# Weight halves that are stationary, interleaved column by column, and begun at eight places in turn

## The chip, the cores and the metric

The kernel runs on one core of a Trainium2 chip. The metric is the time of one execution on the device in microseconds (us); of several runs the median is given. Matrix products run on TensorE (PE in the profile, with its weight loads as PEld), elementwise work on VectorE (DVE), ScalarE (ACT) and GpSimd (POOL), and transfers are issued from SyncE's queue (SP) and GpSimd's.

## The reference, cut to what matters

Two transformer-like blocks run on 512 tokens of width 2048, in fp32: the first has differential attention and a state-space branch, the second has two layers with neighbourhood, dilated and memory attention. Nearly all arithmetic is in products of the activations with large weights:

```python
# first block, once
h = rms_norm(x, ln_gain[l])
proj = h @ w_in[l]                                # 512 x 2048 times 2048 x 10240
q, k, v, z_att, u, z_ssm, g_att, g_ssm = jnp.split(proj, splits, axis=-1)
...                                               # attention, S5 scan
return y * jax.nn.sigmoid(y @ w_glu + b_glu)
...
merged = (jax.nn.sigmoid(g_att) * (y_att @ w_proj_att[l])
          + jax.nn.sigmoid(g_ssm) * (y_ssm @ w_proj_ssm[l]))
x = x + merged @ w_out[l]

# second block, two layers, on x and on mem (256 rows)
h = rms_norm_2(x, norm_g[l])
z = h @ w_in[l]                                   # 2048 x 7168
...                                               # three kinds of attention, gates
x = x + y @ w_out[l]
```

## The kernel before, in words

Activations lie transposed in SBUF, 16 tiles of 128 features by 512 tokens. Each is kept as two halves in the type fp32r: a high half that the type holds exactly, and the rest as a low half. Weights are split in the same way, and a product of a weight block and an activation tile is three matmuls into one PSUM tile (`mm3`, lines 183 to 185): high by high, high by low, low by high.

Weights come in units (`wunit`): four blocks of 128 rows by 256 columns, one DMA of 512 KB into `raw` (line 196), a cast to the high half on ScalarE (`split`, line 189) and a subtraction for the low half on VectorE (line 190), both over 1,024 elements in each of 128 partitions. The result is `hl`, in a ring of three buffers; a buffer holds 2,176 elements and the halves take 2,048 of them, so that the place where they begin (`at`, in bytes) can be chosen. The high halves of all four blocks lie first, and the low halves behind them: a row of a block is 256 elements without a gap. A unit is asked for ahead of time by the scheduler's priority, and begins when the matmuls on the unit three before it have given their buffer back.

Two kinds of product use the units. In `gemm_t` the weight is the stationary operand, in pieces of 128 columns, and the activations move, 512 columns (256 where the memory of 256 rows is the activation); the result comes out transposed, in two PSUM tiles `pg`. In `gemm_tok` the activations are stationary and the weights move, 256 columns at a time. Both go through `accumulate`, which takes the units one after the other; a unit of `gemm_t` is 4 blocks x 2 pieces x 3 = 24 matmuls. The constants `AT_T, AT_MEM, AT_TOK = 256, 64, 448` say where in the buffer the halves begin for 512 columns, for the memory's 256, and for `gemm_tok`.

Between the matmuls of these products, `tick` lets pieces of other work in by a count that is written in the code (`SSM_EVERY`, `ATT_EVERY` and such): attention scores (L848, L849), transposes of weights of attention (L1132), sums of squares by a matmul with a constant (L779, stationary `blk64` and `onesE`), and the state-space branch. Its scan (63 steps of five small VectorE instructions, L564 to L568) runs beside products with `w_in`. What the change touches is `wunit`, `gemm_t`, `gemm_tok` and `accumulate`.

Of the kernel before, what the change touches and what calls it, by code (L numbers as in the profile page):

```python
# [20 lines left out]
NMEM = 256  # L21
# [22 lines left out]
AT_T, AT_MEM, AT_TOK = 256, 64, 448  # L44
# [73 lines left out]
class Net:  # L118
    def __init__(self, ctx, tc, a):
        self.ctx, self.tc, self.nc, self.a = ctx, tc, tc.nc, a  # L120
        self.n = 0
        self.between = []
        self.ahead = AHEAD_FIRST
        nc = self.nc
        cp = ctx.enter_context(tc.tile_pool(name="const", bufs=1))
        self.cp = cp
        self.ident = self.const("ident", [P, P])
        self.onesD = cp.tile([P, P], F32, name="onesD")
        nc.vector.memset(self.onesD, 1.0 / D)
        self.col = ctx.enter_context(tc.tile_pool(name="col", bufs=16))  # L130

        line = ctx.enter_context(tc.tile_pool(name="line", bufs=1, side="right"))
        line.tile([P, 120], F32, name="line")
        self.wr = ctx.enter_context(tc.tile_pool(name="wr", bufs=3))
        self.wh = ctx.enter_context(tc.tile_pool(name="wh", bufs=3))
        self.tmp = ctx.enter_context(tc.tile_pool(name="tmp", bufs=8))
        self.nrm = ctx.enter_context(tc.tile_pool(name="nrm", bufs=2))
        self.pg = ctx.enter_context(tc.tile_pool(name="pg", bufs=4, space=PSUM))
        self.pa = ctx.enter_context(tc.tile_pool(name="pa", bufs=2, space=PSUM))
        self.dram = ctx.enter_context(tc.tile_pool(name="scratch", bufs=1, space=DRAM))  # L140
# [48 lines left out]
        self.nc.scalar.copy(hi, src)  # L189
        self.nc.vector.tensor_sub(lo, src, hi.bitcast(F32))  # L190

    def wunit(self, src, k0, kk, c0, cw=256, pool=None, at=0):

        with self.tc.high_priority(self.ahead):
            raw = self.wr.tile([P, 4, 256], F32, tag="raw", name=self.nm("raw"))[:, :kk, :cw]
            self.nc.sync.dma_start(out=raw, in_=src[k0 * P:(k0 + kk) * P, c0:c0 + cw].rearrange("(k p) c -> p k c", p=P))
            hl = (pool or self.wh).tile([P, 2176], FR, tag="hl", name=self.nm("hl"), bufs=4 if pool else 3)
            hl = hl[:, at // 4:at // 4 + 2048].rearrange("p (h k c) -> p h k c", h=2, k=4)[:, :, :kk, :cw]
            self.split(hl[:, 0], hl[:, 1], raw)
        return hl  # L200

# [21 lines left out]
    def gemm_t(self, src, c0, mov, n=T):  # L223

        out = [self.psg()[:, :n] for _ in range(2)]

        def step(hl, k, kk, i, first, last):
            x = mov[k]
            c = slice(i * P, (i + 1) * P)
            self.mm3(out[i], hl[:, 0, kk, c], hl[:, 1, kk, c], x[:, 0], x[:, 1], first, last)  # L230

        return self.accumulate(src, c0, len(mov), out, step, AT_MEM if n == NMEM else AT_T)

    def gemm_tok(self, src, c0, mov, nt):

        out = [self.psg()[:, :256] for _ in range(nt)]

        def step(hl, k, kk, i, first, last):
            x = mov[k]
            t = slice(i * P, (i + 1) * P)  # L240
            self.mm3(out[i], x[:, 0, t], x[:, 1, t], hl[:, 0, kk], hl[:, 1, kk], first, last)

        return self.accumulate(src, c0, len(mov), out, step, AT_TOK)

    def accumulate(self, src, c0, kt, out, step, at):


        n = len(out)
        for ku in range(0, kt, 4):
            hl = self.wunit(src, ku, 4, c0, at=at)  # L250
            order = [(k, i) for k in range(4) for i in range(n)]
            if ku == 0:
                order.sort(key=lambda o: o[1] // 2)
            if ku == kt - 4:
                order.sort(key=lambda o: o[1])
            for k, i in order:
                step(hl, ku + k, k, i, ku + k == 0, ku + k == kt - 1)
                self.tick(1.0 / n)
        return out
# [1008 lines left out]
```

## Time and profile before

| what | value |
|---|---|
| median of 3 runs | 3312.57 us (3311.8 to 3313.15) |
| the profiled execution's own time | 3314.32 us |
| its span, first to last instruction | 3312.3 us |
| TensorE matmuls busy | 3275.6 us (99%), 17,844 instructions |
| TensorE weight loads busy | 2823.8 us (85%) |
| VectorE busy | 1753.0 us (53%) |
| ScalarE busy | 1174.2 us (35%) |
| GpSimd busy | 293.3 us (9%) |
| DMA | 410.11 MB, 124 GB/s on average |

The profile is of one execution. Busy time counts an engine as occupied while any instruction of it runs; matmuls are pipelined and overlap, so the duration of one is longer than the distance from its start to the next one's, and it is the distances that add up to the span. Rows name the engine, the line of the kernel, and the tiles by the program's names: `pg<-xg,hl` is a matmul into `pg` with moving operand `xg` and stationary `hl`.

### The profile page before, as it was taken

What the parts mean: (1) busy time and instruction counts of PE and PEld (TensorE: products, weight loads), DVE (VectorE), ACT (ScalarE), POOL (GpSimd) and SP (SyncE); (2) the same over time, 40 slices, a digit from 0 to 9 for tenths busy, and PEclk for the clock granted to TensorE, in tenths of its full rate; (3) what the DMA queues carried; (4) which work ended last, traced back from release to release, by engine and by line L of the source; (5) the groups of instructions that cost most, each with busy time, mean ns of one, the idle gap of its engine ahead of it and who ended that gap; (6) DMA issues with size and microseconds to landing.
All of it is one profiled execution on the core that took longest, in us unless ns stands there. A gap on an engine that the chain in (4) does not pass through costs nothing.

```text
span 3312.3 us, 44959 instructions
## 1 busy us (share of the span) xinstructions
PE 3275.6 (99%) x17844; PEld 2823.8 (85%) x17844; DVE 1753.0 (53%) x3227; ACT 1174.2 (35%) x1851; POOL 293.3 (9%) x426
## 2 busy tenths in 40 slices
PE   8999999999999999999999999999999999999998
PEld 6998877888888788888888888888888888888898
DVE  5464486445888754434444556443354455554433
ACT  4432222243555432223333334323343333343333
POOL 3200001311111000011011000001101100000000
PEclk9999999999999999999999999999999999999999
DMA  6564443454333354344333222334443332233433
GB/s 222 180 199 120 130 123 121 135 187 134 100 101 96 110 186 146 124 141 153 99 98 94 90 87 76 127 122 132 147 138 96 95 93 86 83 97 123 137 113 111
DMA packets 365954, 410.11 MB, mean 124 GB/s; under 512 B 36506, under 2 KB 327209, under 8 KB 365616
## 3 DMA queue, kind: packets, MB, share of 16 engines
q1 hardware_dynamic: 350800, 363.73, 35.4%
q0 software_dynamic: 14944, 43.52, 3.7%
q8 instruction: 140, 2.29, 0.3%
q14 instruction: 70, 0.57, 0.1%
HBM read 355.86 MB, written 47.70 MB: 122 GB/s over the span
## 4 chain that ended last, share of the span: by engine, by line
PE 94%; DVE 3%; DMA 1%; issue 1%; ACT 0%; POOL 0%; SPq 0%; ACTq 0%; DVEq 0%; POOLq 0%
PE pg L183 29%; PE pg L185 28%; PE pg L184 28%; PE pa L1132 1%; PE pa L184 1%; PE pa L185 1%; PE pa L183 1%; DVE hl L190 1%; PE pa L584 0%; DVE s L565 0%; DVE s L566 0%; DVE s L567 0%; DVE st L568 0%; DVE s L564 0%; PE pa L779 0%
## 5 line engine op out<-in xcount | busy, mean ns | idle before, releaser
L190 DVE TENSOR_TENSOR hl<-raw,hl 128x1024 fp32r<-128x1024 f32 x552 | 680.8, 1234 | 943.9 <-ACT hl L189 942.4
L183 PE MATMUL pg<-xg,hl 128*128 128x512 f32 (+1 forms) x2688 | 1069.7, 398 | 0.0
L185 PE MATMUL pg<-xg,hl 128*128 128x512 f32 (+1 forms) x2688 | 1039.9, 387 | 8.8 <-DVE hl L190 8.8
L184 PE MATMUL pg<-xg,hl 128*128 128x512 f32 (+1 forms) x2688 | 1038.1, 386 | 0.0
L189 ACT CAST hl<-raw 128x1024 fp32r<-128x1024 f32 x552 | 578.9, 1050 | 1074.5 <-PE pg L185 890.5
L185 PEld LDWEIGHTS pg<-xg,hl 128*128 128x128 f32 x2688 | 505.6, 188 | 115.2 <-DVE hl L190 13.8
L183 PEld LDWEIGHTS pg<-xg,hl 128*128 128x128 f32 x2688 | 507.4, 189 | 87.7 <-ACT xg L312 0.4
L184 PEld LDWEIGHTS pg<-xg,hl 128*128 128x128 f32 x2688 | 507.7, 189 | 80.4
L183 PE MATMUL pg<-hl,xg 128*128 128x256 f32 x1152 | 327.4, 284 | 0.0
L185 PE MATMUL pg<-hl,xg 128*128 128x256 f32 x1152 | 322.3, 280 | 0.0
L184 PE MATMUL pg<-hl,xg 128*128 128x256 f32 x1152 | 322.2, 280 | 0.0
L184 PE MATMUL pg<-yh,hl 128*128 128x512 f32 x576 | 224.3, 389 | 0.0
L185 PE MATMUL pg<-yh,hl 128*128 128x512 f32 x576 | 224.3, 389 | 0.0
L183 PE MATMUL pg<-yh,hl 128*128 128x512 f32 x576 | 224.3, 389 | 0.0
L185 PEld LDWEIGHTS pg<-hl,xg 128*128 128x128 f32 x1152 | 219.0, 190 | 0.0
L183 PEld LDWEIGHTS pg<-hl,xg 128*128 128x128 f32 x1152 | 217.0, 188 | 1.5
L184 PEld LDWEIGHTS pg<-hl,xg 128*128 128x128 f32 x1152 | 216.7, 188 | 1.6
L183 PE MATMUL pg<-hl,yh 128*128 128x256 f32 x512 | 145.7, 285 | 0.0
L190 DVE TENSOR_TENSOR wt<-pa,wt 128x512 fp32r<-128x512 f32 (+3 forms) x144 | 83.1, 577 | 118.2 <-ACT wt L189 117.7
L185 PE MATMUL pg<-hl,yh 128*128 128x256 f32 x512 | 143.7, 281 | 0.0
L184 PE MATMUL pg<-hl,yh 128*128 128x256 f32 x512 | 143.6, 281 | 0.0
L189 ACT CAST wt<-pa 128x512 fp32r<-128x512 f32 (+3 forms) x144 | 71.3, 495 | 166.6 <-PE pa L1132 166.2
(282 smaller groups left out, 3983.0 us busy)
## 6 DMA issues: line engine op xcount, KB each, us to landing
raw<-in_w_in_dram SPq DMA_DIRECT2D x384, 512.0 KB, 3.5
raw<-in_w_out_dram SPq DMA_DIRECT2D x96, 512.0 KB, 3.6
raw<-in_w_mem_kv_dram SPq DMA_DIRECT2D x32, 512.0 KB, 4.5
o_d<-t POOLq DMA_DIRECT2D x40, 256.0 KB, 2.3
t<-o_d SPq DMA_DIRECT2D x40, 256.0 KB, 3.9
sg_d<-t POOLq DMA_DIRECT2D x32, 256.0 KB, 2.5
raw<-in_w_proj_att_dram SPq DMA_DIRECT2D x16, 512.0 KB, 3.7
raw<-in_w_proj_ssm_dram SPq DMA_DIRECT2D x16, 512.0 KB, 3.6
```

Of the source, the lines that this page charges most:

```text
L183: mm(ps, wh, xh, start=start, stop=False)
L184: mm(ps, wh, xl, start=False, stop=False)
L185: mm(ps, wl, xh, start=False, stop=stop)
L189: self.nc.scalar.copy(hi, src)
L190: self.nc.vector.tensor_sub(lo, src, hi.bitcast(F32))
L1132: self.nc.tensor.transpose(pt[:, i * P:(i + 1) * P], w, self.ident)
```

## The change

`wunit` gets a parameter `turns`. With it, the two halves of a weight lie in turn: element `2c` of a row is the high half of column `c`, element `2c + 1` the low half, so each half is written and read with a step of two elements, which is 8 bytes. `gemm_t` asks for that, and no longer begins at a constant place: a counter goes up by one with each product, and the halves begin at 32 bytes times the counter modulo eight (0 to 224). All units of one product begin at the same place. `gemm_tok` keeps its layout and its place. Every engine's instructions are the same as before and stand in the same order.

```diff
+        self.units = 0
...
-    def wunit(self, src, k0, kk, c0, cw=256, pool=None, at=0):
+    def wunit(self, src, k0, kk, c0, cw=256, pool=None, at=0, turns=False):
...
             hl = (pool or self.wh).tile([P, 2176], FR, tag="hl", name=self.nm("hl"), bufs=4 if pool else 3)
-            hl = hl[:, at // 4:at // 4 + 2048].rearrange("p (h k c) -> p h k c", h=2, k=4)[:, :, :kk, :cw]
+            hl = hl[:, at // 4:at // 4 + 2048]
+            if turns:
+                hl = hl.rearrange("p (k c h) -> p h k c", k=4, h=2)[:, :, :kk, :cw]
+            else:
+                hl = hl.rearrange("p (h k c) -> p h k c", h=2, k=4)[:, :, :kk, :cw]
             self.split(hl[:, 0], hl[:, 1], raw)
...
-        return self.accumulate(src, c0, len(mov), out, step, AT_MEM if n == NMEM else AT_T)
+        self.units += 1
+        return self.accumulate(src, c0, len(mov), out, step, 32 * (self.units % 8), True)
...
-        return self.accumulate(src, c0, len(mov), out, step, AT_TOK)
-
-    def accumulate(self, src, c0, kt, out, step, at):
+        return self.accumulate(src, c0, len(mov), out, step, AT_TOK, False)
+
+    def accumulate(self, src, c0, kt, out, step, at, turns):
...
-            hl = self.wunit(src, ku, 4, c0, at=at)
+            hl = self.wunit(src, ku, 4, c0, at=at, turns=turns)
```

## Rows read from the trace of the kernel before

**Rows 1.** The page: busy time, TensorE's granted clock, the chain by engine.

```profile
span 3312.3 us, 44959 instructions
PE 3275.6 (99%) x17844; PEld 2823.8 (85%) x17844; DVE 1753.0 (53%) x3227; ACT 1174.2 (35%) x1851; POOL 293.3 (9%) x426
PEclk9999999999999999999999999999999999999999
PE 94%; DVE 3%; DMA 1%; issue 1%; ACT 0%; POOL 0%; SPq 0%; ACTq 0%; DVEq 0%; POOLq 0%
```

**Rows 2.** Groups by shape: count | busy us, mean ns of one | idle before.

```profile
L184 PE MATMUL pg<-xg,hl 128*128 128x512 f32 x2560 | 1002.4, 392 | 0.0
L184 PEld LDWEIGHTS pg<-xg,hl 128*128 128x128 f32 x2688 | 507.7, 189 | 80.4
L185 PE MATMUL pg<-yh,hl 128*128 128x512 f32 x576 | 224.3, 389 | 0.0
L183 PE MATMUL pg<-m,hl 128*128 128x512 f32 x256 | 99.7, 390 | 0.0
L183 PE MATMUL pg<-xg,hl 128*128 128x256 f32 x128 | 35.8, 280 | 0.0
```

**Rows 3.** Timeline of TensorE, undisturbed: first and last of 14 matmuls.

```profile
743.91 0.39 PE L183 MATMUL pg<-yh,hl 128*128 128x512 f32 x1
...
746.86 0.39 PE L184 MATMUL pg<-yh,hl 128*128 128x512 f32 x1
```

**Rows 4.** Timeline of TensorE behind two matmuls of 256 columns (start us, us, what).

```profile
1002.50 0.40 PE L183 MATMUL pg<-xg,hl 128*128 128x512 f32 x1
...
1003.66 0.40 PE L185 MATMUL pg<-xg,hl 128*128 128x512 f32 x1
1003.89 0.63 PE L779 MATMUL pa<-t,r_onesE 128*128 128x512 f32 x2
1004.36 0.29 PE L848 MATMUL pa<-k,q 128*128 128x256 f32 x1
```

**Rows 5.** Timeline of TensorE: first and last of 16 and of 31 matmuls.

```profile
1706.51 0.28 PE L185 MATMUL pg<-hl,xg 128*128 128x256 f32 x1
...
1708.21 0.28 PE L185 MATMUL pg<-hl,xg 128*128 128x256 f32 x1
...
890.44 0.28 PE L183 MATMUL pg<-hl,xg 128*128 128x256 f32 x1
...
893.98 0.28 PE L183 MATMUL pg<-hl,xg 128*128 128x256 f32 x1
```

**Rows 6.** Timeline of TensorE: matmuls of 128 columns.

```profile
889.12 0.28 PE L184 MATMUL pa<-wt,v 128*128 128x128 f32 x1
889.23 0.27 PE L185 MATMUL pa<-wt,v 128*128 128x128 f32 x1
```

**Rows 7.** Lines 189, 190, 657, 706, 658: ns min/median/max, first and last start.

```profile
L189 ACT CAST hl<-raw x552: 1029/1051/1068, 11.7 to 3266.6; 128x1024 fp32r<-128x1024 f32 x184
L190 DVE TENSOR_TENSOR hl<-raw,hl x552: 1198/1226/2037, 12.9 to 3267.7; 128x1024 fp32r<-128x1024 f32 x184
L657 DVE TENSOR_TENSOR t<-t,y x8: 684/690/693, 734.6 to 771.5; 128x512 f32<-128x512 f32 x8
L706 DVE TENSOR_TENSOR t<-t,pg x16: 1121/1130/1139, 1375.4 to 1532.7; 128x512 f32<-128x512 f32 x16
L658 DVE TENSOR_TENSOR t<-t,t x8: 1167/1173/1177, 735.4 to 772.2; 128x512 f32<-128x512 f32 x8
```

**Rows 8.** Stretches: length, busy us and counts; then line 190 alone.

```profile
424.00:535.00 111.00, 102.24 (x439) 81.14 (x438) 103.67 (x366) 22.86 (x27) 7.96 (x11) 1.00 0.38 118
800.00:1130.00 330.00, 327.81 (x1908) 286.23 (x1907) 267.69 (x623) 185.49 (x352) 43.56 (x46) 1.00 0.33 99
...
424.00:535.00 111.00, 22.49 (x19) 1.00 0.38 118
800.00:1130.00 330.00, 74.65 (x81) 1.00 0.33 99
```

## The prediction

> **What bounds the kernel now.** I read the page first. TensorE has work for 3275.6 us of a span of 3312.3 us, its granted clock is full in every slice, and the chain that ended last is 94% TensorE [rows 1]. So the time is the number of matmuls times the distance from one start to the next. The second view is therefore the groups by shape: the `pg` products of `gemm_t` are 2,560 + 576 + 256 matmuls of 512 columns on each of three lines, 10,176 in all, and the products on the memory are 128 on each line, 384 in all, of 256 columns [rows 2]. The other 256-column products (`gemm_tok`) have the activations as stationary operand; the change doesn't touch their layout.
>
> The third view is the timeline, for starts. In an undisturbed stretch 13 steps take 2.95 us, 226.9 ns each [rows 3]; durations (389 to 390 ns there, [rows 2]) overlap and are no price. The reader is to see that the same instructions can run slower with nothing missing: right after two 256-column matmuls of the attention, five steps of `gemm_t` take 1.16 us, 232 ns each, and the two of L779 behind them take 0.47 us, 235 each [rows 4]. No engine is waited for there. `gemm_tok` shows it more plainly: 15 steps in 1.70 us (113 ns) in one place, 30 steps in 3.54 us (118 ns) in another, with the same shapes [rows 5]. So there is a cost of some 5 ns that depends on how a matmul and the weight load beside it stand to each other, and a product can be in step (227 or 113) or out of step (232 or 118). That the two reads meet in SBUF is my reading of it; the rows show only the two levels.
>
> In step is where long stretches are now. The groups give the share roughly: the 512-column matmuls on L184 have a mean of 392 ns where attention work is mixed in (`pg<-xg,hl`) and 389 to 390 where none is (`pg<-yh,hl`, `pg<-m,hl`) [rows 2]. I take 2.5 ns as what the mixed ones pay today, and nothing for the others.
>
> **The change, part by part.** Every engine runs the same instructions in the same order before and after; only addresses differ. Three things can cost or give.
>
> (1) How the weight load stands to the moving operand. Today the stationary tile begins at 256 bytes in its buffer for all 512-column products, and the built addresses put stationary and moving operand a multiple of 64 bytes apart in every such matmul. Afterwards the place moves on by 32 bytes with each product, so in half of them the two are 32 bytes off that, and in all of them the load walks 8 bytes a column in place of 4. The trace has no load with a step. What it has of the offset is small: the stationary tiles of L779 lie 32 bytes off by their addresses, and their steps are the 235 ns above, though a short matmul or two stands close by and could be the reason. Bounds: nothing, if each product still finds its step; 232 − 227 = 5 ns each, if none does; a gain of 2.5 ns for the mixed 7,680, if the new walk never gets out of step. I take the middle by the L779 rows: the half that lies 32 bytes off runs out of step. That is 3,840 mixed matmuls at 5 − 2.5 = 2.5 ns, 9.6 us, and 1,248 others at 5 ns, 6.2 us: **+16 us**. The bounds are −19 us (7,680 × 2.5 ns) and +32 us (twice the above).
>
> (2) The weight load's own time. It shows as the distance between matmuls too short to hide it: the 128-column ones of `wt,v` follow each other at 0.11 us [rows 6]. Under a 512-column matmul (227 ns) a load may double and still cost nothing, so the cover is some 113 ns; if it is gone, each further 10 ns cost 10,176 × 10 ns = 102 us. Under the 384 memory matmuls of 256 columns (113 ns) there is no cover: they cost 0 if the load keeps its time and 384 × 113 ns = 43 us if it doubles. The nearest rows are loads without a step, so I take it as unchanged, and 5 ns for half of the 384: **+1 us**.
>
> (3) The split that writes the halves. ScalarE writes the high half and VectorE subtracts, 1,051 and 1,226 ns [rows 7], now both with a step of 8 bytes (VectorE also reads with it). No row has that step. VectorE rows with a step of 32 bytes on one or more operands take 1,130 and 1,173 ns for 512 elements, where the same without a step takes 690 [rows 7]: 440 ns more, so 880 ns for the 1,024 elements of a split. That is the upper bound for either engine; the lower is nothing. At a quarter of that step I take a quarter of the price, 220 ns. In dense stages it is hidden: a unit of four k-blocks is 24 matmuls, 5.4 us, against 2.3 us of split (4.0 at the bounds), and a unit may begin two units ahead. It isn't hidden in the scan, from 424 to 535 us. There VectorE is busy 103.7 of 111 us and TensorE 102.2, with 19 subtractions in it [rows 8]; behind a longer one queue the scan's small steps and the next product's weights, and TensorE waits for those. 19 × 220 ns is **+4 us** (0 to 17 us). The next most loaded stretch, 800 to 1130 us, has VectorE at 267.7 of 330 us with 81 subtractions [rows 8]; at 220 ns that is 286, still free, and at 880 ns 339, which would be 9 us over: kept for the range.
>
> [...]
>
> Sum: 16 + 1 + 4 = +21 us on the profiled execution's own 3314.3 us, 3335 us. That execution is 0.05% above the median of the runs shown (3312.57), so in terms of the median 3333 to 3334. I say **3333 us**, 0.6% slower; this likeliest case has 3320 to 3345 for its own.
>
> **The rivals.**
> *No product falls out of step (chance 0.27).* If a product finds its step within a few matmuls wherever it begins, part (1) is nothing and the time is 3313 us, to 3319 with the scan's 4 us and a little. For it: after the disturbance the timeline comes back to 227 by itself, so the step isn't given by the addresses alone. Against it: `gemm_tok` stays at 118 for 30 steps in [rows 5] with the same addresses modulo 64. [...]
>
> *Faster: the walk of 8 bytes never meets the moving operand for long (chance 0.22).* If what is paid out of step comes from two reads that go along side by side, a load at another pace gets past, and the matmuls behind each attention piece run at 227 at once. The mixed 7,680 then give back up to 19 us: 3295 us, and 3305 if the splits take some of it. It decides from the point where the five steps in [rows 4] fall under 229 ns. For it: the excess is there only when something shorter stands just ahead. Against it: a walk at another pace may also meet the other read in every matmul.
>
> *Slower still: every product out of step (chance 0.12).* Part (1) is 32 us, and with the splits at their bound in the scan 17 more: 3345 to 3365 us.
>
> *The load with a step takes twice its time or more (chance 0.03).* The memory products alone then cost 43 us: with the rest 3370 us, and far more if it passes 227 ns. Nothing in this trace speaks for it, and nothing excludes it.
>
> **How the numbers follow.** My forecast has 0.36. The range, 3297 to 3368 us, runs from the faster case nearly to its bound to the slower ones, and leaves out some 0.05 below and 0.08 above. 0.2% is 6.6 us, about what a measurement of this kernel can tell from no change. Faster than 3306: 0.22. Within it: 0.28, the no-change case and the lowest edge of my forecast. Slower: 0.50.
>
> **What would show it.** In the changed profile, undisturbed products (`yh`, `m`) alternate: one at 227 ns a step, the next at about 232; if all stay at 227, part (1) is wrong and a rival holds. After attention pieces the steps show whether the walk helps. LDWEIGHTS of `pg` stays at 188 to 189 ns if (2) holds. [...] What would make it wrong altogether: that the 227 itself holds a cost of the two reads, which would go. Then each ns gives 10 us, and the time leaves the range below.

## The result, and the profile after

The changed kernel takes 3358.97 us (median of 3 runs, 3356.95 to 3361.0), before 3312.57: 1.4% slower, ratio 1.0142 with a 95% interval of 1.0127 to 1.0156. The forecast was 3333 us; the time lies in the range and has the forecast sign, but the loss is 46 us where 21 were forecast.

The page of the changed kernel: busy time, and the chain by engine.

```profile
span 3354.9 us, 44959 instructions
PE 3323.8 (99%) x17844; PEld 2893.2 (86%) x17844; DVE 1756.2 (52%) x3227; ACT 1205.6 (36%) x1851; POOL 292.2 (9%) x426
...
PE 94%; DVE 3%; DMA 1%; issue 1%; ACT 0%; POOL 0%; SPq 0%; DVEq 0%; ACTq 0%; POOLq 0%
```

TensorE's busy time has grown by 48 us with the same 17,844 matmuls, the chain is the same as in [rows 1], and VectorE is where it was. So matmuls follow each other more slowly, and TensorE waits for no other engine more than it did. The groups by shape (count, busy us, mean ns of one, idle before) answer to [rows 2]; lines have moved on by one:

```profile
L186 PE MATMUL pg<-xg,hl 128*128 128x512 f32 x2560 | 1012.9, 396 | 7.1 <-DVE hl L191 7.1
L185 PE MATMUL pg<-xg,hl 128*128 128x512 f32 x2560 | 1011.9, 395 | 0.0
L185 PEld LDWEIGHTS pg<-xg,hl 128*128 128x128 f32 x2688 | 526.0, 196 | 75.8
L184 PE MATMUL pg<-m,hl 128*128 128x512 f32 x256 | 101.0, 395 | 0.0
L184 PE MATMUL pg<-xg,hl 128*128 128x256 f32 x128 | 36.3, 284 | 0.0
```

The mixed matmuls read 395 to 396 ns instead of 392, the undisturbed ones 395 instead of 390, and no shape of `gemm_t` has escaped. The weight load reads 196 instead of 189.

The product `w_out` of the first block shows it place by place: its activations are `m`, nothing else runs on TensorE beside it, and its eight products of 96 matmuls take the eight places in turn. The timeline of the changed kernel, first matmul of each product, and the very last one:

```profile
1371.27 0.39 PE L184 MATMUL pg<-m,hl 128*128 128x512 f32 x1
...
1393.66 0.39 PE L184 MATMUL pg<-m,hl 128*128 128x512 f32 x1
...
1416.07 0.39 PE L184 MATMUL pg<-m,hl 128*128 128x512 f32 x1
...
1438.47 0.39 PE L184 MATMUL pg<-m,hl 128*128 128x512 f32 x1
...
1460.87 0.39 PE L184 MATMUL pg<-m,hl 128*128 128x512 f32 x1
...
1483.14 0.40 PE L184 MATMUL pg<-m,hl 128*128 128x512 f32 x1
...
1505.23 0.40 PE L184 MATMUL pg<-m,hl 128*128 128x512 f32 x1
...
1527.63 0.40 PE L184 MATMUL pg<-m,hl 128*128 128x512 f32 x1
...
1549.62 0.39 PE L186 MATMUL pg<-m,hl 128*128 128x512 f32 x1
```

By the addresses of the built program, these products lie 160, 192, 224, 0, 32, 64, 96 and 128 bytes from the moving operand, modulo 256. That is where the high half begins; the low half lies 4 bytes further on. Each difference over 96 (the last over 95) is the distance from start to start: 233, 233, 233, 233, 232, 230, 233 and 231 ns. Before, `w_out` took 226.7 ns a step in every product; its first and last of 768 matmuls in the kernel before:

```profile
1356.18 0.39 PE L183 MATMUL pg<-m,hl 128*128 128x512 f32 x1
...
1530.04 0.39 PE L185 MATMUL pg<-m,hl 128*128 128x512 f32 x1
```

The reader is to see that there is no alternation: all eight places lose, the one at 0 as much as any.

Behind the 256-column matmuls of the attention the prediction wanted to see whether the steps get shorter. In the changed kernel, first and last of six matmuls behind such a pair:

```profile
1010.76 0.40 PE L184 MATMUL pg<-xg,hl 128*128 128x512 f32 x1
...
1011.93 0.39 PE L186 MATMUL pg<-xg,hl 128*128 128x512 f32 x1
```

Five steps take 1.17 us, 234 ns each, against 232 in [rows 4]. The first steps were long before the change too. What has changed is that they don't end: the sixth step behind such a pair had a median of 226 ns over the kernel before, and has 232 in the changed one.

The splits, lines 190 and 191 (ns min/median/max over all 552), answer to [rows 7]:

```profile
L190 ACT CAST hl<-raw x552: 1034/1120/1167, 11.7 to 3310.7; 128x1024 fp32r<-128x1024 f32 x184
L191 DVE TENSOR_TENSOR hl<-raw,hl x552: 1200/1226/2780, 12.9 to 3311.8; 128x1024 fp32r<-128x1024 f32 x184
```

ScalarE's writes with a step of 8 bytes cost some 70 ns (1,120 against 1,051), VectorE's nothing (1,226 in both). In the scan (424 to 535 us; the row gives length, then TensorE, its loads, VectorE) VectorE is busy 103.47 us of 111 where it was 103.67, and TensorE is idle for 7.1 us where it was for 8.8 [rows 8].

```profile
424.00:535.00 111.00, 103.93 (x440) 84.45 (x439) 103.47 (x366) 25.36 (x28) 7.91 (x11) 1.00 0.36 115
```

Summing the distances from each start to the next over both traces, by tile: `xg` with 512 columns 1809.0 us before and 1839.0 after, `yh` 391.7 and 401.9, `m` 174.1 and 178.6, the memory products 44.5 and 46.3, `gemm_tok` 592.3 and 588.0. That is +30.0 + 10.2 + 4.5 + 1.8 − 4.3 = +42.2 us, and the span of the profiled execution has grown by 42.6.

### The profile page after: what moved, and what is told of

Its sections match the earlier page's. It is cut to its first block, busy times and chain, and to the rows that moved or that the text cites. A ratio compares the mean times of both kernels' runs of the same rounds, so it can differ in the third digit from the quotient of the medians.

```text
span 3354.9 us, 44959 instructions
## 1 busy us (share of the span) xinstructions
PE 3323.8 (99%) x17844; PEld 2893.2 (86%) x17844; DVE 1756.2 (52%) x3227; ACT 1205.6 (36%) x1851; POOL 292.2 (9%) x426
## 4 chain that ended last, share of the span: by engine, by line
PE 94%; DVE 3%; DMA 1%; issue 1%; ACT 0%; POOL 0%; SPq 0%; DVEq 0%; ACTq 0%; POOLq 0%
PE pg L184 29%; PE pg L186 28%; PE pg L185 28%; PE pa L1139 1%; PE pa L185 1%; PE pa L184 1%; PE pa L186 1%; DVE hl L191 1%; PE pa L591 0%; DVE s L573 0%; DVE st L575 0%; DVE s L572 0%; DVE s L574 0%; DVE s L571 0%; PE pa L786 0%
## 5 line engine op out<-in xcount | busy, mean ns | idle before, releaser
L190 ACT CAST hl<-raw 128x1024 fp32r<-128x1024 f32 x552 | 611.7, 1109 | 1098.2 <-PE pg L186 918.4
L186 PEld LDWEIGHTS pg<-xg,hl 128*128 128x128 f32 x2688 | 525.2, 195 | 106.3 <-DVE hl L191 11.8
L184 PEld LDWEIGHTS pg<-xg,hl 128*128 128x128 f32 x2688 | 525.9, 196 | 82.9 <-DVE v L320 1.1
L185 PEld LDWEIGHTS pg<-xg,hl 128*128 128x128 f32 x2688 | 526.0, 196 | 75.8
L184 PE MATMUL pg<-yh,hl 128*128 128x512 f32 x576 | 227.3, 395 | 0.0
L185 PE MATMUL pg<-yh,hl 128*128 128x512 f32 x576 | 227.3, 395 | 0.0
L186 PE MATMUL pg<-yh,hl 128*128 128x512 f32 x576 | 227.2, 394 | 0.0
```

What stands on the lines that cost most here:

```text
L184: mm(ps, wh, xh, start=start, stop=False)
L185: mm(ps, wh, xl, start=False, stop=False)
L186: mm(ps, wl, xh, start=False, stop=stop)
```

## The experiments

**Step alone.** The halves in turn, at the constant places of before:

```diff
-        return self.accumulate(src, c0, len(mov), out, step, 32 * (self.units % 8), True)
+        return self.accumulate(src, c0, len(mov), out, step, AT_MEM if n == NMEM else AT_T, True)
```

> Halves in turn (step of 8 bytes), but all products begin at the constant places of before. Theory (the step does it: the weight load takes longer and leaves its step with the moving operand wherever it begins): 3352 to 3364 us, ratio 1.012 to 1.016, LDWEIGHTS of pg at 195 to 196 ns, undisturbed products at 232 to 233 ns from start to start. Rival (the places do it, the half of them that lies 32 bytes off, as the prediction had it): 3309 to 3320 us, 227 ns undisturbed.

Measured: 3369.11 us, ratio to the kernel before 1.0168 (1.0153 to 1.0184). The undisturbed product, first and last of 768 matmuls:

```profile
1377.29 0.39 PE L184 MATMUL pg<-m,hl 128*128 128x512 f32 x1
...
1556.26 0.39 PE L186 MATMUL pg<-m,hl 128*128 128x512 f32 x1
```

178.97 us over 767 steps is 233.3 ns. Halves in turn are enough, with the high half at the very place that is in step without a step. One thing comes with the step that this run can't tell from it: the low half, one load in three, begins 4 bytes further on. The matmuls beside a high half (lines 184 and 186, 233.0 and 233.4 ns) are as slow as those beside a low half (line 185, 233.6), but a disturbance lasts for about five steps in the kernel before (the sixth is at 226 ns), so one load in three could be enough. This kernel even loses some 10 us more than the full change, which has places at 230 to 232 ns among its eight. The loads are at 193 to 194 ns, a little less than expected.

**Places alone.** The eight places, the halves one behind the other as before:

```diff
-        return self.accumulate(src, c0, len(mov), out, step, 32 * (self.units % 8), True)
+        return self.accumulate(src, c0, len(mov), out, step, 32 * (self.units % 8), False)
```

> Halves one behind the other as before (no step), but the eight places in turn. Theory of the step: 3309 to 3320 us, every undisturbed product at 227 ns, LDWEIGHTS at 188. Rival (places): 3350 to 3362 us if all places lose, about 3333 with products alternating between 227 and 232 ns if those 32 bytes off lose.

Measured: 3349.99 us, ratio 1.0112 (1.0097 to 1.0127). The theory that only the step counts falls. The same eight products of `w_out`, first matmul of each and the last:

```profile
1368.73 0.40 PE L184 MATMUL pg<-m,hl 128*128 128x512 f32 x1
...
1391.14 0.40 PE L184 MATMUL pg<-m,hl 128*128 128x512 f32 x1
...
1413.12 0.40 PE L184 MATMUL pg<-m,hl 128*128 128x512 f32 x1
...
1435.51 0.39 PE L184 MATMUL pg<-m,hl 128*128 128x512 f32 x1
...
1457.28 0.39 PE L184 MATMUL pg<-m,hl 128*128 128x512 f32 x1
...
1479.67 0.40 PE L184 MATMUL pg<-m,hl 128*128 128x512 f32 x1
...
1502.07 0.39 PE L184 MATMUL pg<-m,hl 128*128 128x512 f32 x1
...
1524.55 0.39 PE L184 MATMUL pg<-m,hl 128*128 128x512 f32 x1
...
1546.62 0.40 PE L186 MATMUL pg<-m,hl 128*128 128x512 f32 x1
```

At distances of 160, 192, 224, 0, 32, 64, 96 and 128 bytes modulo 256 the starts are 233, 229, 233, **227**, 233, 233, 234 and 232 ns apart. One place of eight is in step, and 192 loses a third; 64 and 128 are hardly better than their neighbours. So either part of the change alone loses most of what both lose, or a little more (1.1% and 1.7%, both together 1.4%): they don't add up, as there is one thing to lose, being in step, and either takes it away.

**One other place.** The kernel before, with one constant changed, so that nothing rotates and nothing has a step:

```diff
-AT_T, AT_MEM, AT_TOK = 256, 64, 448
+AT_T, AT_MEM, AT_TOK = 320, 64, 448
```

> The kernel before with one constant changed: the halves of the 512-column products begin at 320 bytes in place of 256, so that stationary and moving operand are 64 bytes apart modulo 256, and no longer 0. Theory (only a distance of 0 modulo 256 is in step, a multiple of 64 is not enough): 233 to 234 ns undisturbed, about 3365 to 3375 us, ratio 1.016 to 1.018. Rival (going from place to place costs, not the place): 227 ns, 3309 to 3319 us. Rival (the prediction's premise, any multiple of 64 is in step): the same 3309 to 3319 us.

Measured: 3362.61 us, ratio 1.0153 (1.0138 to 1.0168), a little under the band expected. `w_out` again:

```profile
1371.97 0.39 PE L183 MATMUL pg<-m,hl 128*128 128x512 f32 x1
...
1550.93 0.40 PE L185 MATMUL pg<-m,hl 128*128 128x512 f32 x1
```

178.96 us over 767 steps, 233.3 ns. Going from place to place costs nothing by itself (places alone had 227 ns at a distance of 0); the place does.

**Distance or place.** Two kernels with the padding tiles shortened, which moves the stationary and the moving operands together to 192 modulo 256; the second has the constant 320 as well, which puts the stationary one back at 0:

```diff
-        line.tile([P, 120], F32, name="line")
+        line.tile([P, 120 - 48], F32, name="line")
...
-        cp.tile([P, 88], F32, name="fill")
+        cp.tile([P, 88 - 16], F32, name="fill")
```

> The kernel before with every buffer behind the two padding tiles moved to 192 bytes modulo 256 (64 bytes less padding on one side of SBUF, 192 on the other), stationary and moving operand of the 512-column products alike, so that they are still 0 apart. Theory (what counts is the distance of the two operands modulo 256): 227 ns undisturbed and 3309 to 3320 us. Rival (what counts is where the stationary operand lies by itself): 229 ns, as for the products at 192 in the run with the places alone, and about 3325 to 3335 us.

> The same, and the halves begin at 320 bytes in place of 256: the stationary operand lies at 0 modulo 256 as in the kernel before, the moving one at 192, 64 apart. Theory (distance): 233 ns undisturbed, 3358 to 3372 us. Rival (place of the stationary operand): 227 ns, 3309 to 3320 us.

Measured: 3311.94 us, ratio 0.9998 (0.9989 to 1.0008), for the first; 3362.21 us in one run for the second. Of the first only the time is read. The second's `w_out`:

```profile
1373.29 0.40 PE L183 MATMUL pg<-m,hl 128*128 128x512 f32 x1
...
1552.26 0.39 PE L185 MATMUL pg<-m,hl 128*128 128x512 f32 x1
```

Again 233.3 ns, with the stationary operand just where it is in step in the kernel before. What counts in these runs is the distance between the operands modulo 256 (233.3 ns at 64, and at 0 the time of before, 3311.94 us), not where either lies.

**Larger steps.** Constant places; in one kernel the four blocks' columns in turn (16 bytes), in the other blocks and halves (32 bytes):

```diff
-                hl = hl.rearrange("p (k c h) -> p h k c", k=4, h=2)[:, :, :kk, :cw]
+                hl = hl.rearrange("p (h c k) -> p h k c", k=4, h=2)[:, :, :kk, :cw]   # 16 bytes
+                hl = hl.rearrange("p (c k h) -> p h k c", k=4, h=2)[:, :, :kk, :cw]   # 32 bytes
```

> Constant places; the four blocks' columns lie in turn, so the stationary operand has a step of four elements (16 bytes). The change made the load 7 ns longer with twice the bytes walked. If a load's length goes with the bytes walked, LDWEIGHTS goes to about 209 ns (three times 7 over 188) and the memory products of 256 columns lose 20 ns each. If out of step is one level that any such walk falls to: 232 to 233 ns undisturbed, 3360 to 3370 us. If each stretch of bytes walked costs the matmul again (6 ns per further 512 bytes): 245 ns, about 3490 us.

> Constant places; blocks and halves in turn, a step of eight elements (32 bytes). Length by bytes walked: LDWEIGHTS about 237 ns, still under a 512-column matmul, memory products 160 ns in place of 113 (18 us). One level: 232 to 233 ns undisturbed, 3370 to 3385 us. Cost by bytes walked: 269 ns, about 3740 us. VectorE and ScalarE write with 32 bytes between elements: 880 ns more a subtraction if the rows L658 and L706 carry over, up to 17 us in the scan on top of either.

Measured: 3552.9 us (ratio 1.0726, 1.071 to 1.0742) and 3656.4 us (1.1036, 1.1018 to 1.1055). None of the scales that I had written down fits. At 16 bytes the load is 310 ns, not 209, and the memory products (256 columns, no cover) read 397 to 400 ns in place of 280; groups by shape:

```profile
L185 PEld LDWEIGHTS pg<-yh,hl 128*128 128x128 f32 x576 | 178.3, 310 | 0.0
...
L184 PE MATMUL pg<-xg,hl 128*128 128x256 f32 x128 | 51.2, 400 | 0.0
```

The splits in the same kernel:

```profile
L190 ACT CAST hl<-raw x552: 1032/2055/2148, 12.5 to 3504.4; 128x1024 fp32r<-128x1024 f32 x184
L191 DVE TENSOR_TENSOR hl<-raw,hl x552: 1217/2042/3568, 14.5 to 3505.5; 128x1024 fp32r<-128x1024 f32 x184
```

and at 32 bytes:

```profile
L190 ACT CAST hl<-raw x552: 1031/2215/2492, 11.7 to 3610.6; 128x1024 fp32r<-128x1024 f32 x184
L191 DVE TENSOR_TENSOR hl<-raw,hl x552: 1217/2243/3585, 13.9 to 3611.7; 128x1024 fp32r<-128x1024 f32 x184
```

So it isn't bytes walked: from 4 to 8 bytes a column hardly anything changes (load 188 to 193, cast 1,050 to about 1,120, subtraction 1,226 to 1,226), from 8 to 16 everything jumps (117 ns on the load, the splits to two thirds more or about double), and from 16 to 32 the load (310 to about 330 ns) and the splits grow by a tenth or less. In these runs the jump lies between 8 and 16 bytes alike for reads by TensorE's load, for writes by ScalarE and for VectorE's subtraction, which reads and writes with the step. Why it lies there isn't shown. Under a 512-column matmul the steps are 235 ns (180.24 us over 767 steps of `w_out`):

```profile
1517.20 0.40 PE L184 MATMUL pg<-m,hl 128*128 128x512 f32 x1
...
1697.44 0.39 PE L186 MATMUL pg<-m,hl 128*128 128x512 f32 x1
```

The 233 ns of being out of step and these 235 are not the same thing. The memory products of the same kernel, half as wide, go at the same pace; first and last of 22 matmuls:

```profile
149.88 0.40 PE L184 MATMUL pg<-xg,hl 128*128 128x256 f32 x1
...
154.83 0.40 PE L184 MATMUL pg<-xg,hl 128*128 128x256 f32 x1
```

4.95 us over 21 steps is 236 ns, where these products have a mean of 116 before. As 256 and 512 columns take the same time, 236 and 235 ns, I take the pace for that of the load, the one thing they share that got longer (188 to 310 ns): by the memory products it has about doubled, from 116 to 236 ns, and used up its cover, which is the prediction's rarest rival. At 32 bytes `w_out` is at 244 ns. Of the 237 us by which the span grew at 16 bytes, 156 lie in the mixed products, 20 ns a matmul where undisturbed ones lost 8. VectorE and ScalarE have 16% of that kernel's chain, where they had 3%; how much of the loss is waiting for the splits isn't shown.

**Shorter loads.** To see whether the cost goes with the columns loaded, three kernels load 32 columns in place of 128, which leaves out three quarters of the rows of the shortened products. The first shortens one matmul in three, at the constant 320:

```diff
+            mm, s = self.nc.tensor.matmul, slice(i * P, i * P + 32)
+            mm(out[i], hl[:, 0, kk, c], x[:, 0], start=first, stop=False)
+            mm(out[i][:32], hl[:, 1, kk, s], x[:, 0], start=False, stop=False)
+            mm(out[i], hl[:, 0, kk, c], x[:, 1], start=False, stop=last)
```

> As the kernel with the constant 320, but of the three matmuls of a weight piece the one with the low half of the weight loads 32 columns of it in place of 128 (it leaves out three quarters of that small term) and stands in the middle. Theory (the cost comes from the weight load beside the matmul): a 512-column matmul that runs beside the short load takes 227 to 229 ns, the other two kinds 233 to 234. Rival (the place slows the matmul itself, whatever is loaded beside it): all three kinds 233 to 234. If the 227 of the kernel before still holds a cost of the load, those beside the short load fall under 225.

Measured in one run: 3346.05 us. The timeline of `w_out`, first and last of 10 matmuls, with the one behind the first:

```profile
1399.81 0.40 PE L231 MATMUL pg<-m,hl 128*128 128x512 f32 x1
1400.05 0.39 PE L232 MATMUL pg<-m,hl 128*32 128x512 f32 x1
...
1401.89 0.40 PE L231 MATMUL pg<-m,hl 128*128 128x512 f32 x1
```

Nine steps take 2.08 us, 231 ns each, and the one beside the short load (from 1399.81) is the slowest, 0.24 us. Over all of `w_out` the steps behind the three lines are 234, 230 and 229 ns. The theory expected the opposite, so a short load doesn't spare the matmul beside it; the two beside full loads are the ones that got shorter. The second and third kernel shorten all three matmuls in 14 of 16 k-blocks, at the constant 320 and at 256:

```diff
+            if first or last or n == NMEM:
+                self.mm3(out[i], hl[:, 0, kk, c], hl[:, 1, kk, c], x[:, 0], x[:, 1], first, last)
+            else:
+                s = slice(i * P, i * P + 32)
+                self.mm3(out[i][:32], hl[:, 0, kk, s], hl[:, 1, kk, s], x[:, 0], x[:, 1], False, False)
```

> Constant 320 again, and in the 512-column products 14 of the 16 (or 6 of the 8) k-blocks load 32 columns of the weight in place of 128 in all three matmuls (it leaves out three quarters of the products' rows in those blocks). Theory (the cost is met by the load beside the matmul, in proportion to the columns loaded): the excess over 227 falls from 6.7 to a quarter, 228 to 229 ns undisturbed, and not under 226.5. Rival 1 (the place itself slows the moving operand): 233 ns still. Rival 2 (the 227 also holds a cost of the load): well under 226, 216 to 222.

> The constant of before (256), with 32 columns loaded in place of 128 in 14 of 16 k-blocks (it leaves out three quarters of the products' rows there). Two readings of why a load with a step never gets in step. If it needs only the right distance: 227 ns with short loads too. If it needs a load that lasts as long as it does now: 229 to 232 ns, as with short loads at the constant 320. Under 226 would mean that the 227 holds a cost of the load.

Measured in one run each: 3336.3 and 3333.78 us. The undisturbed `yh` product, first at 320 (13 matmuls), then at 256 (19):

```profile
741.13 0.40 PE L183 MATMUL pg<-yh,hl 128*32 128x512 f32 x1
...
743.91 0.40 PE L183 MATMUL pg<-yh,hl 128*32 128x512 f32 x1
```

```profile
741.22 0.39 PE L183 MATMUL pg<-yh,hl 128*32 128x512 f32 x1
...
745.39 0.39 PE L183 MATMUL pg<-yh,hl 128*32 128x512 f32 x1
```

2.78 us over 12 steps and 4.17 over 18: 232 ns in both. The cost doesn't shrink to a quarter with a quarter of the columns, and at 256, the good place, short loads lose the step too. So the right distance is needed and not enough: of the loads tried at this distance, only the one of before, 128 columns without a gap, is in step. No undisturbed 512-column product, with any load, had a mean under 226.7, so no run shows that the 227 holds a cost of the load.

**The other shape.** Sixteen places in turn for `gemm_tok`, where the weight moves, in place of the constant 448:

```diff
-        return self.accumulate(src, c0, len(mov), out, step, AT_TOK)
+        self.toks += 1
+        return self.accumulate(src, c0, len(mov), out, step, 32 * (self.toks % 16))
```

> The kernel before, with 16 places 32 bytes apart in turn for the products in which the weight moves (256 columns), in place of the constant 448. It shows which distance of the two operands these products want. Theory (each shape has a narrow distance in step, and the constant of before is a good one): mean of these products up from 117 to 118 or 119 ns, 3315 to 3330 us, with some place at 113 all the way through. Rival (they are bound by the load and no place matters): 3309 to 3319 us and no place differs by more than 1 ns.

Measured: 3318.6 us, ratio 1.0021 (1.0012 to 1.0031). The distances of these products add up to 597.7 us where they were 592.3, so other places lose a little. The four products that nothing interrupts have means of 115 to 119 ns at their places, so the place matters, but none is at 113. Nor does the constant of before give that each time: there one such product is at 113 ns and three at 118. What sets their step isn't found.

## Why the prediction was wrong

**That a product is in or out of step, at some 5 ns a matmul, and that this is what the change touches: right.** 233.3 against 226.7 ns, with the chain as it was, is what [rows 3 to 5] showed in small. The price, 6.6 ns, was read a little low, 232 − 227, from a stretch that was coming back into step.

**Which products fall out: the step that failed.** "I take the middle by the L779 rows: the half that lies 32 bytes off runs out of step." All fall out. There were two errors. The rows of L779 stand behind short matmuls, as the prediction noted, and carried no weight. And the premise behind the other half, that a multiple of 64 bytes is what the kernel before had, was read from an address that is also a multiple of 256 in all 10,176 matmuls: places alone show 227 ns at 0 and 232 to 233 at 64 and 128. So seven places of eight lose without the step already (1.1%), and with it all eight. The term was 16 us; measured are 30.0 on the mixed matmuls (3.9 ns each, 2.5 for half of them were forecast) and 14.7 on the others, 44.7. All products out of step at the prediction's own prices would have been 32 us, twice its term; the other 13 us are the price.

**The weight load: nearly right.** It was taken as unchanged and grew by 5 to 7 ns, but under a 512-column matmul that doesn't show: the steps are 233.3 ns with a load of 188 ns at the constant 320, and 233.3 with one of 193 at a step of 8 bytes. The memory products, which the prediction gave no cover, lost 1.8 us where 1 was forecast.

**The splits: too dear.** VectorE's subtraction costs nothing more at 8 bytes (1,226 ns as before), so the scan lost nothing where 4 us were forecast: TensorE's idle time there fell from 9 us to 7. ScalarE's cast costs some 70 ns and is hidden (ScalarE has 0% of the chain). A quarter of the 32-byte price was an interpolation over what is a jump between 8 and 16 bytes (1,226 ns at 4 and at 8 bytes, 2,042 at 16). The bound for 32 bytes, 880 ns, was a little low: the subtraction took 1,017 ns more.

**The rivals.** "Every product out of step", at 0.12, was the one that happened, with 3345 to 3365 us. That its time fits is partly luck: it had up to 17 us from the splits, which cost nothing, and a step at 5 ns, which cost 6.6. "No product falls out of step" had for it that the timeline comes back to 227 by itself: it does, but of the eight places only at a distance of 0. "Faster" falls with the steps behind the attention, which were to come under 229 ns and are 234, and with the mixed matmuls, which are 3 to 4 ns longer in the groups.

**What stays open.** Of the eight distances tried only 0 modulo 256 is in step (227 ns), and halves in turn lose it there (233), as 32-column loads do (232). Whether the halves in turn lose it by the step of 8 bytes or by the low half's 4 bytes wasn't tried; a kernel with the step and every second element left empty would tell. Why either of them, or a shorter load, loses it isn't shown. That two reads of SBUF meet was my reading and isn't shown: a quarter of the columns loaded left more than two thirds of the cost (232 ns, where 227 is in step and 233 is not), which a cost for every meeting would not. A distance of 64 bytes between TensorE's two operands was worth 50 us here (3362.61 against 3312.24); by what mechanism isn't shown.

## What to carry to other kernels

Where TensorE is busy all the time, compare the distance from start to start of identical matmuls across stretches: two levels for one shape (227 and 233 ns here) can mean that operand addresses cost something (a shorter matmul ahead gives a second level too, for about five steps here), and one constant in the layout was worth 1.5%. Measure such a thing with a product per place in one kernel, as the eight products of `w_out` did, before a layout is changed. A layout with a step of 8 bytes in fp32 was cheap here for the engines that read or write it (TensorE's load 188 to 193 ns, the cast 1,051 to 1,120, the subtraction 1,226 in both), and one of 16 dear (310, 2,055 and 2,042); but for the stationary operand halves in turn cost 1.7%, as its matmuls fell out of step.

## What was not expected of the hardware

Of the eight distances tried between stationary and moving operand of a 512-column fp32r matmul, only 0 bytes modulo 256 is in step: 226.7 ns there, 229 at 192, and 232 to 234 at the other multiples of 32. The same matmuls with a 32-column load take 232 ns at either of the two places tried, more than with the full load at the good one. And a step of 16 bytes takes the load from 188 to 310 ns, where 8 bytes take it to 193, and then products of 256 and of 512 columns go at one pace, 235 to 236 ns.
